# Start addresses at multiples of 64 bytes and three row pitches for the projection's operands

## The chip, the cores and the metric

One core of one Trainium2 chip runs the whole kernel. The metric is the device time of one execution in microseconds (us); the median of three runs of the kernel before is 1004.42 us, the lowest 1004.33, the highest 1007.7.

## What is computed

One decoder layer over 1040 positions (16 learned meta tokens, then 1024 tokens) of width 1024. Cut to what matters:

```python
h = rms_norm(h_res, pre_norm_g[i])
z = h @ w_in[i]                       # 1040 x 1024 times 1024 x 7328
(pv, pg, cq, ckv, kr, mg, cu, cg, sbcx, sg, gl) = split_cols(z)
y_a = (pool_mixer(pv, ...) * silu(pg)) @ w_out_pool[i]
y_b = (mla_attention(cq, ckv, kr, ...) * silu(mg)) @ w_out_mla[i]
y_c = (conformer_conv(cu, ...) * silu(cg)) @ w_out_conf[i]
y_d = (short_conv(sbcx, ...) * silu(sg)) @ w_out_sc[i]
m = sum(sigmoid(gate_k) * y_k)        # four gates out of gl
h_res = h_res + rms_norm(m @ w_o[i], post_norm_g[i])
return h_res[:, N_META:]
```

## The kernel before

All large products are done in float32r on numbers split into a high and a low part: each operand has a hi and a lo copy, and a product is three matmuls, hi by hi, hi by lo and lo by hi.

**The projection (first 650 us or so).** `h @ w_in` is done with a Winograd scheme of seven half-size products (28 pairs of column blocks, 256 columns each). The activations stand in seven operand tiles `HB[b]` of shape 128 x 2 x 4 x 528: 2 for hi and lo, 4 blocks of 128 channels (`k`), and a row of 528 columns, 512 tokens and 16 meta columns. A row is thus 2112 bytes. The seven are B11, B21, B22 (= a block of h), T1, T2, T4 (sums of blocks) and T3, which is also the block B12. The second half of the tokens has no meta tokens of its own, so the 16 meta columns of B22 and of T3 are filled with zeros by two memsets on POOL, right at the start. `product` streams one row of `HB[b]` at a time past a block of weights: for each `k` the three matmuls are (hi weights, hi row), (hi weights, lo row), (lo weights, hi row), so 12 in all.

`unit` does the seven products of one pair of column blocks into the PSUM banks `ps_pa` to `ps_pd`. 23 of the 28 pairs need the 1024 tokens alone and run it once with 512 columns. Five need the meta columns too (the list marks them `MT`); they run it twice, on columns 0 to 255 (256 of them) and on columns 256 to 527 (272). `plain` does the block `ckv`/`kr` without the scheme, in the same two stretches: for each of two halves of the tokens `j` and two column blocks `i`, two products of 12 matmuls.

**The attention (about 650 to 873 us)** runs eight heads in two halves of the queries; `ps_s` are the scores, `ps_o` the weighted sums, and between them the output products of three branches (`ps_y`) are put in as filler. `maxima` first computes the scores of one head with a block of 128 queries as weights, streaming the keys `kt` in pieces: 656 keys go in two pieces of 328, 784 in two of 392, 912 in two of 456. **The end (873 us on)** is the output product of the attention branch (`ps_u<-boM`) and the Winograd product with `w_o` (`ps_o`, `ps_u` with the tiles `wa` streaming).

**Order and places.** Nothing is issued when it is written down. Every operation is recorded (`Plan.record`, which is why nearly all lines of the profile say L330, the line from which all is issued) and put in order by a list scheduler, `Plan.flush`, with a cost for each operation; a matmul of n columns in float32r costs `max(108, n / 2.25 + 3)` ns there. A buffer that will lie where an earlier one lay may be written only after the earlier one's last use (`sl["after"]`, from `Plan.lay_out`).

`Pool.lay_out` gives every buffer its place in a partition's memory. Buffers of the pools on the left follow each other from byte 512 of the kernel's own area up, those on the right (`HB` in the projection, the tiles `cp` later) end at byte `SBUF` = 212832. Each buffer's size is rounded up to 32 bytes. Since 212832 = 3325 x 64 + 32 and the sizes on the right are all multiples of 64, the right side starts half of 64 bytes off a multiple of 64; on the left the constants take 736 bytes, and everything behind them starts at 512 + 736 = 1248 = 19 x 64 + 32. The area itself starts at a multiple of 64. So nearly all operands lie at 32 bytes past a multiple of 64. Exceptions are the identity matrix, some buffers of the last stage that lie behind a 32-byte tile (`rso`): `a`, `c11`, `c22`, `u2`, `g`, and slices that start at an odd column.

Of the kernel before, what the change touches and what calls it, by code (L numbers as in the profile page):

```python
# [21 lines left out]
F32 = mybir.dt.float32  # L22
F32R = mybir.dt.float32r
BF16 = mybir.dt.bfloat16
AF = mybir.ActivationFunctionType
ALU = mybir.AluOpType
# [4 lines left out]
P = 128  # L31
# [5 lines left out]
KH = KD // 2  # L37

SBUF = 212832
# [5 lines left out]
LH = 512 + NM  # L45
# [11 lines left out]
B11, B21, B22, T1, T2, T3, T4 = range(7)  # L57
# [7 lines left out]
def f(ap):  # L65
    return ap.bitcast(F32)
# [79 lines left out]
class Pool:  # L146
# [30 lines left out]
    def lay_out(self, start):  # L177

        for g in self.groups.values():
            g["one"] = -(-max(b.bytes for b in g["order"]) // 32) * 32  # L180
        size = sum(g["n"] * g["one"] for g in self.groups.values())
        at = start = start - size if self.space == "right" else start
        for tag, g in self.groups.items():
            if not g["slots"]:
                g["slots"] = [{"i": i, "live": None, "after": 0} for i in range(g["n"])]
                for sl in g["slots"]:
                    self.pool.tile([P, g["one"] // 4], F32, tag=f"{tag}_{sl['i']}", name=f"{tag}_{sl['i']}")
            for sl in g["slots"]:
                sl["place"] = (self.space, at, at + g["one"])
                at += g["one"]  # L190
        return start if self.space == "right" else at


# [242 lines left out]
def trunk_kernel(ctx, tc, a):  # L436
    nc = tc.nc
    plan = Plan(nc)
    PE, ACT, DVE, POOL, SP = (plan.engine(e) for e in ("PE", "ACT", "DVE", "POOL", "SP"))
    ctx.enter_context(tc.manual_schedule())  # L440

    def pool(stack, **kw):
        return plan.open(stack, Pool(plan, stack.enter_context(tc.tile_pool(bufs=1, **kw)),
                                     psum=kw.get("space") == PSUM,
                                     side="dram" if kw.get("space") == DRAM else kw.get("side", "left")))
# [4 lines left out]
    def copy(out, in_, scale=1.0):  # L450
        ACT.activation(out, in_, AF.Copy, scale=scale)

    def sub(eng, out, x, y):
        eng.tensor_tensor(out, x, y, op=ALU.subtract)
# [7 lines left out]
    def split(hi, lo, src, eng=None):  # L462
        copy(hi, src)
        sub(eng or POOL, lo, src, f(hi))
# [10 lines left out]
    def rsqrt_mean(out, ssq, n, eps=EPS):  # L475

        DVE.tensor_scalar(out, ssq, 1.0 / n, eps, op0=ALU.mult, op1=ALU.add)
        POOL.tensor_tensor(out, out, mhalf[:out.shape[0], :out.shape[1]], op=ALU.pow)
# [29 lines left out]
    one = ExitStack()  # L508
    hpool = pool(one, name="hb", side="right", reuse_waits="tile")
    HB = {}  # L510
    for b, name in ((B11, "B11"), (T2, "T2"), (T1, "T1"), (T3, "T3"), (B21, "B21"), (T4, "T4"), (B22, "B22")):
        HB[b] = hpool.tile([P, 2, KH, LH], F32R, name=name)
    psum = pool(one, name="psum1", space=PSUM, reuse_waits="tile")

    def bank(tag="x"):

        return psum.tile([P, 512], F32, tag=tag, bufs=2 if tag == "x" else 1, name=f"ps_{tag}")
# [45 lines left out]

    def product(ps, w, b, c0, n, start, stop):

        for k in range(KH):
            s = slice(c0, c0 + n)
            xh, xl = HB[b][:, 0, k, s], HB[b][:, 1, k, s]
            last = stop and k == KH - 1
            PE.matmul(ps, w[:, 0, k], xh, start=start and k == 0, stop=False, skip_group_check=True)  # L570
            PE.matmul(ps, w[:, 0, k], xl, start=False, stop=False, skip_group_check=True)
            PE.matmul(ps, w[:, 1, k], xh, start=False, stop=last, skip_group_check=True)
# [3 lines left out]
    def unit(w, c0, n, out, pump, early=False):  # L576
# [10 lines left out]
        def first():  # L587
            product(pa, w["A12"], B21, c0, n, False, True)
            with plan.ahead(EVAC):
                out(0, 0, pa, None, u3 if early else a_)  # L590
            pump()

        product(pa, w["A11"], B11, c0, n, True, True)
        with plan.ahead(EVAC):
            copy(a_, pa)
        pump()
        if early:
            first()
        product(pb, w["S2"], T2, c0, n, True, True)
        with plan.ahead(EVAC):  # L600
            add(DVE, u2, pb, a_)
# [19 lines left out]
    def plain(w, c0, n, out):  # L621

        for j, bs in enumerate(((B11, B21), (B12, B22))):
            for i, m in enumerate((P, 64)):
                ps = bank(("pa", "pb")[i])[:m, :n]
                for h, b in enumerate(bs):
                    product(ps, w[h][i], b, c0, n, h == 0, h == 1)
                with plan.ahead(EVAC):
                    out(i, j, ps, None, None)
# [8 lines left out]
    def pairs_of_halves(n, each, store):  # L638

        z = {}  # L640

        def out(i, j, ps, x, tmp):
            first = i not in z
            if first:
                z[i] = up.tile([P, 2, n], F32, tag="z", bufs=2, name="z")
            m = ps.shape[0]
            each(i, z[i][:m, j], ps, x, tmp)
            if not first:
                store(i, z[i][:m])
        return out  # L650
# [79 lines left out]
    def square(x_, t):  # L730
        n = x_.shape[0]
        ACT.activation(tp.tile([P, D], BF16, tag="whl", name="junk")[:n], x_, AF.Square, accum_out=ssx[:n, t:t + 1])

    def scaled(x_, t):
        n = x_.shape[0]
        for i in range(2):
            s = slice(512 * i, 512 * (i + 1))
            DVE.scalar_tensor_tensor(x_[:, s], x_[:, s], rsx[:n, t:t + 1], gB[i][:n], op0=ALU.mult, op1=ALU.mult)
# [35 lines left out]
    def meta():  # L774
        square(xm, 8)
        rsqrt_mean(rsx[:NM, 8:9], ssx[:NM, 8:9], D)
        scaled(xm, 8)
        pt = bank()
        for k in range(KD):
            PE.transpose(pt[:, NM * k:NM * (k + 1)], xm[:, P * k:P * (k + 1)], ident[:NM, :NM])  # L780
        b1, b2 = (pt[:, 64 * i:64 * (i + 1)].rearrange("p (k n) -> p k n", n=NM) for i in range(2))
        hm = up.tile([P, 2, KH, NM], F32, tag="a", name="hm")
        copy(hm[:, 0], b1)
        sub(DVE, hm[:, 1], b2, hm[:, 0])
        for b, src, eng in ((B11, b1, DVE), (B21, b2, DVE), (T2, b1, DVE), (T4, hm[:, 1], DVE)):
            split(HB[b][:, 0, :, 512:], HB[b][:, 1, :, 512:], src, eng)
        hi = HB[T1][:, 0, :, 512:]
        copy(hi, b1, scale=-1.0)
        DVE.scalar_tensor_tensor(HB[T1][:, 1, :, 512:], b1, -1.0, f(hi), op0=ALU.mult, op1=ALU.subtract)

    for b in (B22, T3):
        POOL.memset(f(HB[b][:, :, :, 512:]), 0.0)
    rows = [
        (R_GB, 32, a["gate_bias"][0].rearrange("(k p) -> k p", p=P)),
        (R_PS, 2, a["pool_scale"][0].rearrange("(k p) -> k p", p=P)),
# [24 lines left out]
    parts(2)  # L820
    parts(3)
    meta()
    plain(w_kv, *U0, out_kv[0])
    for t in range(2):
        sums_of(t)
# [3 lines left out]
    for t in range(2, 4):  # L829
        sums_of(t)  # L830
    plain(w_kv, *U1, out_kv[1])
    for t in range(2, 4):
        operand_of(T3, t, xt[t + 4][:, :512])
# [420 lines left out]
    at = pool(two, name="at", reuse_waits="tile")  # L1254
# [324 lines left out]
    for d in (0, 4, 1, 5, 2, 6, 3, 7):  # L1579
# [3 lines left out]
        for c in range(2):  # L1583
            t = th[:, 512 * c:512 * (c + 1)]
            py = bank("u")
            for k in range(4):
                b = boM[c][k]
# [20 lines left out]
    def half(name, bufs=4):  # L1608
        return ep.tile([P, 512], F32, tag=name, bufs=bufs, name=name)
# [71 lines left out]
    for t in range(4):  # L1681

        parts = [slice(0, 512)] if t < 3 else [slice(0, 256), slice(256, 512)]
        g = half("g", 1) if t == 3 else a_[t]
        for i, cols in enumerate(parts):
            ps = bank("u" if i == 0 else "o")[:, cols]
# [43 lines left out]
```

## Time and profile before

| | before |
|---|---|
| time, median of 3 | 1004.42 us |
| profiled execution's own time | 1007.16 us |
| its span | 1005.5 us |
| granted TensorE clock | 0.992 |
| PE busy | 985.0 us, 98% |
| PE weight load busy | 828.5 us, 82% |
| DVE, ACT, POOL busy | 679.9, 445.8, 689.3 us |

PE is TensorE, whose matmuls are records of some 160 ns more than the time from one start to the next, because they are pipelined. What a matmul costs is therefore read from the distance of starts. The profile's chain of work goes back from the last instruction to whatever released each step.

### The profile page before, as it was taken

The numbers are of one execution on the slowest core, as the hardware profiler recorded it, in microseconds if no ns is written. First come the engines' busy times: TensorE is split into PE (matmuls) and PEld (weight loads), VectorE is DVE, ScalarE is ACT, GpSimd is POOL, SyncE is SP. The second block draws the span as 40 slices with busy tenths as digits, with TensorE's granted clock in tenths as the row PEclk, the third lists the DMA queues.
The fourth block names the chain that finished last, engine by engine and source line by source line (L and its number), as shares of the span: only waits on it lengthen the run. The fifth ranks groups of instructions, "written<-read, shape, count | busy, mean of one in ns | idle before, by whom it ended". The sixth has DMA issues, their size and how long they took to land.

```text
span 1005.5 us, 15187 instructions
## 1 busy us (share of the span) xinstructions
PE 985.0 (98%) x5093; PEld 828.5 (82%) x5093; DVE 679.9 (68%) x1106; ACT 445.8 (44%) x895; POOL 689.3 (69%) x640
## 2 busy tenths in 40 slices
PE   9999999999999999999999999989999999999996
PEld 9999898889888888877877888868887888788885
DVE  6856794898699679744454453165777777898547
ACT  7632233343433455444443444215564656224632
POOL 6768767577575698777877666135569796647946
PEclk9999999999999999999999999998999999999999
DMA  7269756568676866866655656795758572773534
GB/s 249 76 203 311 235 168 187 194 190 284 209 265 218 287 210 177 250 198 204 199 165 194 202 155 180 272 268 157 229 149 256 176 232 75 251 251 100 189 100 167
DMA packets 126303, 203.13 MB, mean 202 GB/s; under 512 B 19651, under 2 KB 79162, under 8 KB 124881
## 3 DMA queue, kind: packets, MB, share of 16 engines
q1 hardware_dynamic: 121600, 185.38, 58.9%
q10 hardware_dynamic: 4336, 15.73, 4.1%
q8 instruction: 40, 0.66, 0.3%
q0 software_dynamic: 288, 1.05, 0.3%
q14 instruction: 39, 0.31, 0.1%
HBM read 128.40 MB, written 73.72 MB: 201 GB/s over the span
## 4 chain that ended last, share of the span: by engine, by line
PE 90%; DVE 4%; issue 2%; POOL 2%; DMA 1%; ACT 0%; SPq 0%; DVEq 0%; POOLq 0%; ACTq 0%
PE ps_pb L330 16%; PE ps_pa L330 15%; PE ps_pc L330 15%; PE ps_o L330 10%; PE ps_pd L330 7%; PE ps_u L330 7%; PE ps_s L330 7%; PE ps_y L330 7%; PE ps_x L330 4%; PE ps_w L330 1%; DVE op L330 1%; DMA kt<-kr 1%; DVE ps_w L330 1%; DVE a L330 1%; POOL S L330 0%
## 5 line engine op out<-in xcount | busy, mean ns | idle before, releaser
L330 PE MATMUL ps_pb<-T,S 128*128 128x512 f32 (+2 forms) x792 | 174.8, 363 | 0.1
L330 PE MATMUL ps_pa<-B,A 128*128 128x512 f32 (+2 forms) x792 | 172.8, 362 | 0.0
L330 POOL TENSOR_TENSOR S<-ss,S 128x512 fp32r<-128x512 f32 x84 | 113.6, 1364 | 65.0 <-ACT S L330 59.2
L330 PEld LDWEIGHTS ps_pa<-B,A 128*128 128x128 f32 x792 | 134.6, 188 | 24.4 <-issue 0.7
L330 PEld LDWEIGHTS ps_pb<-T,S 128*128 128x128 f32 x792 | 133.8, 188 | 24.4 <-issue 1.2
L330 POOL TENSOR_TENSOR A<-raw,A 128x512 fp32r<-128x512 f32 x84 | 114.0, 1365 | 49.1 <-ACT A L330 47.0
L330 POOL TENSOR_TENSOR pt<-p,pt 128x512 fp32r<-128x512 f32 (+4 forms) x112 | 102.2, 939 | 51.8 <-ACT pt L330 26.0
L330 DVE SCALAR_TENSOR_TENSOR ps_w<-conv,par,ps_w 128x512 f32<-128x512 f32 x116 | 87.2, 752 | 2.5
L330 PE MATMUL ps_pc<-T,S 128*128 128x512 f32 (+2 forms) x396 | 85.8, 361 | 0.5 <-DVE z L330 0.5
L330 PE MATMUL ps_pc<-B,S 128*128 128x512 f32 (+2 forms) x396 | 85.3, 361 | 0.0
L330 PE MATMUL ps_pd<-T,A 128*128 128x512 f32 (+2 forms) x396 | 84.5, 361 | 0.0
L330 PE MATMUL ps_y<-bo,whl 128*128 128x512 f32 x288 | 83.4, 409 | 0.3 <-DVE op L330 0.3
L330 ACT ACTIVATE p<-ps_s 128x512 f32<-128x512 f32 (+4 forms) x112 | 49.6, 443 | 74.9 <-PE ps_s L330 31.2
L330 ACT ACTIVATE S<-ss 128x512 fp32r<-128x512 f32 x84 | 50.8, 628 | 71.4 <-DVE ss L330 39.3
L330 PEld LDWEIGHTS ps_pd<-T,A 128*128 128x128 f32 x396 | 67.2, 188 | 12.0
L330 PEld LDWEIGHTS ps_pc<-B,S 128*128 128x128 f32 x396 | 67.2, 188 | 12.0
L330 PEld LDWEIGHTS ps_pc<-T,S 128*128 128x128 f32 x396 | 66.9, 188 | 12.3 <-DVE z L330 0.7
L330 PE MATMUL ps_o<-pt,vt 128*128 128x512 f32 (+4 forms) x336 | 75.0, 336 | 1.8 <-ACT ol L330 1.5
L330 PE MATMUL ps_s<-qt,kt 100*128 100x512 f32 (+4 forms) x336 | 68.3, 330 | 0.7 <-DVE qt L330 0.7
L330 ACT ACTIVATE A<-raw 128x512 fp32r<-128x512 f32 x84 | 52.4, 626 | 37.0 <-PE ps_pd L330 18.2
L330 PEld LDWEIGHTS ps_o<-pt,vt 128*128 128x128 f32 (+1 forms) x336 | 53.2, 174 | 16.1 <-ACT ol L330 3.3
L330 PEld LDWEIGHTS ps_s<-qt,kt 100*128 100x128 f32 (+1 forms) x336 | 55.2, 179 | 11.5 <-issue 0.9
(344 smaller groups left out, 1893.8 us busy)
## 6 DMA issues: line engine op xcount, KB each, us to landing
raw<-in_w_in_dram SPq DMA_DIRECT2D x56, 512.0 KB
th<-th SPq DMA_DIRECT2D x32, 512.0 KB
th<-z ACTq DMA_DIRECT2D x30, 512.0 KB
v<-vhl SPq DMA_DIRECT2D x16, 384.0 KB
qt<-q SPq DMA_DIRECT2D x16, 384.0 KB
vt<-v SPq DMA_DIRECT2D x8, 768.0 KB
bo<-bo SPq DMA_DIRECT2D x6, 1024.0 KB
kt<-k SPq DMA_DIRECT2D x8, 520.0 KB
```

The source lines that it names most:

```text
L330: getattr(self.handle[o["eng"]], o["op"])(*map(real, o["args"]), **{k: real(v) for k, v in o["kw"].items()})
```

## The change

Four things are changed.

1. `Pool.lay_out` rounds buffer sizes up to 64 bytes instead of 32, and the right side ends 32 bytes lower (a tile `end` of 32 bytes fills the gap), so that every buffer starts at a multiple of 64 bytes.
2. The rows of `HB[T3]` and `HB[B22]` shrink from 528 to 512 columns (2048 bytes): the zero columns are gone, and with them the two memsets. `product` and `plain` stop at column 512 for these two.
3. The rows of `HB[T1]` and `HB[T2]` grow from 528 to 544 columns (2176 bytes); the added 16 columns are not used. B11, B21 and T4 keep 2112 bytes. The seven tiles together take as many bytes as before.
4. Slices that ran to the end of a row (`512:`) now end at 528 (`512:LH`).

```diff
-            g["one"] = -(-max(b.bytes for b in g["order"]) // 32) * 32
+            g["one"] = -(-max(b.bytes for b in g["order"]) // 64) * 64
         size = sum(g["n"] * g["one"] for g in self.groups.values())
-        at = start = start - size if self.space == "right" else start
+        at = start = start - size - SBUF % 64 if self.space == "right" else start
...
+        if self.space == "right" and not self.base:
+            self.base = self.pool.tile([P, SBUF % 64 // 4], F32, tag="end", name="end")
...
-        HB[b] = hpool.tile([P, 2, KH, LH], F32R, name=name)
+        HB[b] = hpool.tile([P, 2, KH, {T3: 512, B22: 512, T1: 544, T2: 544}.get(b, LH)], F32R, name=name)
...
     def product(ps, w, b, c0, n, start, stop):
 
+        if b in (T3, B22):
+            n = min(n, 512 - c0)
+            ps = ps[:, :n]
...
-                ps = bank(("pa", "pb")[i])[:m, :n]
+                ps = bank(("pa", "pb")[i])[:m, :n if j == 0 else min(n, 512 - c0)]
...
-            each(i, z[i][:m, j], ps, x, tmp)
+            each(i, z[i][:m, j, :ps.shape[1]], ps, x, tmp)
...
-            split(HB[b][:, 0, :, 512:], HB[b][:, 1, :, 512:], src, eng)
+            split(HB[b][:, 0, :, 512:LH], HB[b][:, 1, :, 512:LH], src, eng)
...
-    for b in (B22, T3):
-        POOL.memset(f(HB[b][:, :, :, 512:]), 0.0)
```

More of the change, by code (lines that the diff above doesn't have):

```diff
@@ L785, in meta @@
         for b, src, eng in ((B11, b1, DVE), (B21, b2, DVE), (T2, b1, DVE), (T4, hm[:, 1], DVE)):
-            split(HB[b][:, 0, :, 512:], HB[b][:, 1, :, 512:], src, eng)
-        hi = HB[T1][:, 0, :, 512:]
+            split(HB[b][:, 0, :, 512:LH], HB[b][:, 1, :, 512:LH], src, eng)
+        hi = HB[T1][:, 0, :, 512:LH]
         copy(hi, b1, scale=-1.0)
-        DVE.scalar_tensor_tensor(HB[T1][:, 1, :, 512:], b1, -1.0, f(hi), op0=ALU.mult, op1=ALU.subtract)
-    for b in (B22, T3):
-        POOL.memset(f(HB[b][:, :, :, 512:]), 0.0)
+        DVE.scalar_tensor_tensor(HB[T1][:, 1, :, 512:LH], b1, -1.0, f(hi), op0=ALU.mult, op1=ALU.subtract)
     rows = [
```

## The prediction, made before the changed kernel ran

> **What bounds the kernel now.** I read the page first, then the chain of work that ended last in order of time, then TensorE's timeline in the stretches that the change touches. Two lines of the page:
>
> ```profile
> span 1005.5 us, 15187 instructions
> PE 985.0 (98%) x5093; PEld 828.5 (82%) x5093; DVE 679.9 (68%) x1106; ACT 445.8 (44%) x895; POOL 689.3 (69%) x640
> PE 90%; DVE 4%; issue 2%; POOL 2%; DMA 1%; ACT 0%; SPq 0%; DVEq 0%; POOLq 0%; ACTq 0%
> ```
>
> TensorE is busy for 98% and makes up 90% of the chain, about 905 us; all transfers together are 1% of it. The time changes when a matmul's step changes, or when one of the few places changes where TensorE waits. The chain in order of time has long pieces in which nothing but matmuls stands (start, length, count):
>
> ```profile
> 166.19 2.78 PE ps_pb L330 x12
> 667.20 9.62 DMA kt<-kr
> 873.24 44.62 PE ps_u L330 x192
> 917.86 22.30 PE ps_o L330 x96
> 940.16 22.31 PE ps_u L330 x96
> ```
>
> So a matmul of 512 columns steps by 2.78 / 12 = 231.7 ns in the projection, where rows are 2112 bytes apart, and by 22.31 / 96 = 232.4 ns (44.62 / 192 gives the same) at the end, where rows are 2048 bytes apart. That difference of 0.7 ns is the first hint on row pitch. Both are bound by the streamed row, not by the weights, since the step grows with the columns. This stretch of the timeline has products of 12 matmuls, first with 272 columns (a second stretch of an `MT` pair), then with 256 (the first stretch of the next):
>
> ```profile
> 126.97 1.68 PE L330 MATMUL ps_pb<-T,S 128*128 128x272 f32 x12
> 128.48 1.68 PE L330 MATMUL ps_pc<-T,S 128*128 128x272 f32 x12
> ...
> 134.54 1.68 PE L330 MATMUL ps_pc<-B,S 128*128 128x272 f32 x12
> 136.05 1.58 PE L330 MATMUL ps_pa<-B,A 128*128 128x256 f32 x12
> 137.47 1.58 PE L330 MATMUL ps_pb<-T,S 128*128 128x256 f32 x12
> ```
>
> From 126.97 to 136.05 stand six products of 272 columns (the row of the third to fifth is left out): 9.08 / 6 = 1.513 us each. The one of 256 takes 137.47 - 136.05 = 1.42 us, 118.3 ns a matmul. From 256 to 512 columns a step grows by 231.7 - 118.3 = 113.4 ns, 0.443 ns a column, which leaves about 4.9 ns that do not depend on the columns.
>
> **The meta columns of T3 and B22.** In the second stretch of the five `MT` pairs the products with T3 and B22 stop at 256 columns: 5 x 2 = 10 products. In `plain` it is the second half, two blocks by two column groups: 4 products. Each goes from 1.513 to 1.42 us, so 14 x 0.093 = 1.3 us come off. All of it lies on TensorE's own chain, in stretches such as the one shown where one product starts as the other ends; only the four of `plain`, 0.4 us, lie in the first 50 us, where TensorE also waits for transposes and could lose them again. So -0.9 to -1.3 us; I take -1.3.
>
> **The memsets.** POOL's rows at the start:
>
> ```profile
> 1.37 0.20 POOL L330 MEMSET B<- 128x128 f32 x1
> 1.51 0.20 POOL L330 MEMSET T<- 128x128 f32 x1
> 1.66 0.11 POOL L330 MEMSET conv<- 128x14 f32 x1
> 7.89 0.71 POOL L330 TENSOR_TENSOR rsx<-rsx,mhalf 128x2 f32<-128x2 f32 x1 [6.12 <-DVE rsx L330]
> ```
>
> They take 0.3 us and POOL is idle for 6.12 us behind them, waiting for DVE. Taking them away is worth nothing; without that idle time it would be 0.3 us.
>
> **The row pitch.** 23 full pairs stream 12 matmuls of 512 columns for each operand: 552 for T3 and B22 together, 552 for T1 and T2. T3 and B22 get the pitch of the last stage, 2048 bytes, whose step is 0.7 ns longer: 552 x 0.7 = +0.4 us. A pitch of 2176 bytes occurs nowhere in the trace. Its bounds are the nearest rows: 231.7 ns at 2112 and 232.4 at 2048, so 0 to +0.4 us; nothing excludes a small gain, and I allow the same 0.4 us below. As 2176 steps on from row to row, like 2112 and unlike 2048, I take 0. The engines that write these rows (ACT and DVE, out of the transposes) write the same bytes with another pitch, and their work is hidden behind the wait for x.
>
> **The start addresses.** This is the large question: all 5093 matmuls read operands that move by half of 64 bytes. The trace has both cases side by side. The first piece of the keys in `maxima` starts at the tile's own start, 32 bytes past a multiple of 64; the second starts 328, 392 or 456 columns on, which is 20.5, 24.5 or 28.5 times 64 bytes, and so exactly on a multiple of 64. Three pairs that ran back to back, each with the matmul behind it:
>
> ```profile
> 713.52 0.46 PE L330 MATMUL ps_s<-kt,qt 96*128 96x328 f32 x2
> 713.82 0.40 PE L330 MATMUL ps_y<-bo,whl 128*128 128x512 f32 x1
> ...
> 717.52 0.52 PE L330 MATMUL ps_s<-kt,qt 96*128 96x392 f32 x2
> 717.88 0.55 PE L330 MATMUL ps_s<-qt,kt 100*128 100x272 f32 x3
> ...
> 742.19 0.58 PE L330 MATMUL ps_s<-kt,qt 96*128 96x456 f32 x2
> 742.60 0.52 PE L330 MATMUL ps_s<-qt,kt 100*128 100x144 f32 x6
> ```
>
> The pairs take 0.30, 0.36 and 0.41 us. With 4.9 ns and 0.443 ns a column for both matmuls they would take 0.300, 0.357 and 0.414: the aligned piece is not faster than the other. The streamed row's address therefore costs nothing that this can see, some 3 ns a matmul. What the trace does not hold is a block of weights on a multiple of 64 bytes; there the bound is the 4.9 ns that do not depend on the columns, since the rest is proportional to the streamed columns: 0 to -5093 x 0.0049 = -25 us. I take 0, the row that is nearest.
>
> For the other engines the trace has both cases as well. DVE's convolution slides its start by 4 bytes from tap to tap, through every place within 64 bytes:
>
> ```profile
> L330 DVE SCALAR_TENSOR_TENSOR ps_w<-conv,par,ps_w x116: 733/756/757, 117.6 to 413.5; 128x512 f32<-128x512 f32 x116
> ```
>
> From shortest to longest that is 3%, with the median at the top: the start does not matter. In the last stage ACT squares tiles on multiples of 64 (`c`) and copies tiles off them (`wr`), and POOL multiplies `a` (on) and subtracts into `mh` (off):
>
> ```profile
> L330 ACT ACTIVATE wa<-wr 128x512 fp32r<-128x512 f32 x21 | 13.1, 627 | 13.9 <-DMA wr<-so 8.3 <-PE ps_u L330 3.3 <-POOL c L330 1.5
> L330 ACT ACTIVATE junk<-c 128x512 f32<-128x512 f32 x8 | 5.1, 633 | 6.7 <-DVE c L330 6.6
> L330 POOL TENSOR_TENSOR mh<-m,mh 128x512 fp32r<-128x512 f32 x4 | 5.2, 1295 | 0.0
> L330 POOL TENSOR_TENSOR a<-a,pgB 128x512 f32<-128x512 f32 x3 | 3.9, 1284 | 1.7 <-ACT junk L330 1.7
> ```
>
> 627 against 633 ns and 1295 against 1284: nothing there. For transfers I have no such pair, but TensorE waits for them in one place only (the row of the waits; the page's mean rate and the size of a common load are for a rival below):
>
> ```profile
> PE ps_s L330 <- DMA kt<-kr: 3.3, 1, 3.3
> ...
> DMA packets 126303, 203.13 MB, mean 202 GB/s; under 512 B 19651, under 2 KB 79162, under 8 KB 124881
> ...
> th<-th SPq DMA_DIRECT2D x32, 512.0 KB
> ```
>
> So faster transfers could give back 3.3 us at most, and the start.
>
> **The order.** The planner sees 168 matmuls cheaper by 16 / 2.25 = 7 ns and some places that end a few bytes later, so its list can come out with other neighbours. That costs or gives a little wherever TensorE waits; taken as 0, at most the 3.3 us of that one wait either way as long as no load changes its turn.
>
> [...] The three pairs say that 32 or 64 bytes make no difference. [...]
>
> **The sum.** -1.3 + 0.4 = -0.9 us. The profiled execution took 1007.16 us (span 1005.5, 1.7 around it), 2.7 above the median of 1004.42, within the runs shown (1004.33 to 1007.7). It would become 1006.3; the median 1003.5. Its own range is -1.7 to +0.1 from the columns and the pitch, widened by 3.3 both ways: 999 to 1008. A measurement here can tell about 0.5%, 5 us, from no change; this is inside.
>
> **Rivals.** *Aligned weights shorten each step.* The 4.9 ns go: 1004.4 - 25 = 979. For it speaks that they are not explained by columns; against it that the weights load beside the running matmul. Half of it would give 992. Should the part that grows with the columns fall as well, it would be more than 25 us; the three pairs speak against that for the streamed row. Chance 0.25, most of it between 979 and 999.
>
> *The second head's keys land later.* At the start of the attention the chain shows `kt<-kr`, a load of 9.62 us, and TensorE already waits 3.3 us for its end. Every microsecond by which SP's queue issues it later is then a microsecond of the whole time. If the changed places or the order put one or two loads of 512 KB ahead of it, at 202 GB/s (the page's mean) 2.6 us each, the median becomes 1006 or 1009. It decides from a delay of 6 us, some two such loads and the 0.9 us made good, which gives 1009.5. Chance 0.13 from that point on.
>
> *The change does not do what it says*: an address that stays off a multiple of 64. Then only the columns and pitch count, and the time is the forecast's: not a case of its own.
>
> **How the numbers follow.** Forecast 0.62, the first rival 0.25, the second 0.13. The first lies nearly all below 999.4, the second above 1009.4, the forecast's own range between. So faster 0.25, same 0.61, slower 0.14 (0.01 of the forecast's edge). The range runs from 979, which leaves about half of the first rival out, to 1010, which leaves some 0.08 out.
>
> **What would show it.** Right: products of 12 with 512 columns still at 2.78 us, with T3 and B22 at up to 2.79; ten products of a second stretch at 1.42 instead of 1.51 us; the last stage still at 22.3 us for 96. Wrong: 96 matmuls of the last stage at 21.8 us or less (the first rival, since only addresses changed there), products of T1 or T2 other than those of B11, or a longer wait at `kt<-kr`.

## The result and the profile after

The changed kernel takes 1005.76 us (median of 14 runs, 1002.35 to 1008.58), the kernel before 1006.44 (14 runs beside it; the first three of them gave the 1004.42 that the prediction started from). The ratio is 0.9998, 95% interval 0.9989 to 1.0007: no difference that can be measured. The profiled execution, though, took 1002.35 us against 1007.16 before, and its span is 4.9 us shorter. It is the fastest of the 14, so its own parts have to be read before it is believed. The page, busy times and shares of the chain:

```profile
span 1000.6 us, 15167 instructions
PE 978.3 (98%) x5093; PEld 823.7 (82%) x5093; DVE 687.6 (69%) x1106; ACT 444.5 (44%) x895; POOL 688.9 (69%) x638
PE 84%; DVE 6%; POOL 4%; issue 3%; DMA 2%; ACT 0%; SPq 0%; DVEq 0%; POOLq 0%; ACTq 0%
```

TensorE is still busy for 98%, but its share of the chain fell from 90% to 84%, and DVE, POOL and issue took that over: the chain now runs through places where TensorE waits for others. The chain in order of time (start, length, count):

```profile
193.30 2.80 PE ps_pb L332 x12
...
668.87 8.91 DMA kt<-kr
...
871.01 43.61 PE ps_u L332 x192
914.62 21.76 PE ps_o L332 x96
936.38 21.76 PE ps_u L332 x96
```

Before, the 96 matmuls of the last stage took 22.30 and 22.31 us, now 21.76: 226.7 ns a matmul where it was 232.4. In the projection, 12 matmuls of 512 columns still take 2.78 to 2.80 us on the chain, as before. The second stretches, in TensorE's timeline:

```profile
132.22 1.67 PE L332 MATMUL ps_pd<-T,A 128*128 128x272 f32 x12
133.73 1.60 PE L332 MATMUL ps_pc<-B,S 128*128 128x256 f32 x12
135.17 1.58 PE L332 MATMUL ps_pa<-B,A 128*128 128x256 f32 x12
```

The product of 272 columns takes 133.73 - 132.22 = 1.51 us and the shortened one behind it 135.17 - 133.73 = 1.44. From the waits of TensorE (total, times, longest), four rows; the last three have no counterpart before:

```profile
PE ps_s L332 <- DMA kt<-kr: 2.3, 1, 2.3
...
PE ps_x L332 <- DVE rs L332: 1.1, 1, 1.1
PE ps_y L332 <- DVE pd L332: 0.8, 1, 0.8
PE ps_pb L332 <- DVE u L332: 0.7, 2, 0.4
```

From the starts of the matmuls in the two traces the span divides as follows (us; stalls are what the matmuls of n columns in the projection's scheme take beyond 4.9 + 0.443 n ns, where that is over 14 ns):

| | before | after | difference |
|---|---|---|---|
| projection, from the first matmul on | 650.6 | 652.9 | +2.3 |
| of it: before the first product of the scheme | 53.5 | 52.3 | -1.2 |
| of it: stalls in the scheme | 6.1 | 9.9 | +3.8 |
| of it: the scheme's matmuls of 512 columns, without stalls | 448.0 | 448.6 | +0.6 |
| of it: those of 256 and 272 columns, without stalls | 102.5 | 101.7 | -0.8 |
| attention | 221.0 | 216.4 | -4.5 |
| last stage | 123.0 | 120.2 | -2.8 |

So three things happened. The projection lost 2.3 us though some of its matmuls became shorter, the last stage gained 2.8, and the attention gained 4.5. The attention's part is mostly not the change's: it goes with the granted clock right behind the wait for `kt<-kr`. Stretches of the trace with busy times of PE, PEld, DVE, ACT and POOL, then the granted clock, the DMA share and GB/s, first before:

```profile
674.00:677.00 3.00, 0.06 (x1) 0.09 (x1) 0.71 (x3) 0.00 (x0) 0.95 (x4) 0.87 0.95 263
677.00:680.00 3.00, 3.00 (x11) 2.85 (x12) 0.81 (x3) 0.00 (x0) 0.00 (x0) 0.50 0.74 212
680.00:683.00 3.00, 3.00 (x12) 2.48 (x11) 1.46 (x4) 0.60 (x1) 0.00 (x0) 0.50 0.01 4
683.00:686.00 3.00, 3.00 (x8) 2.32 (x8) 2.78 (x7) 0.80 (x2) 0.00 (x0) 0.50 0.00 0
```

and the changed kernel:

```profile
677.00:680.00 3.00, 2.08 (x8) 2.00 (x9) 0.81 (x3) 0.00 (x0) 0.00 (x0) 0.67 0.96 275
680.00:683.00 3.00, 3.00 (x17) 2.57 (x16) 0.93 (x2) 0.60 (x1) 0.00 (x0) 0.76 0.21 62
683.00:686.00 3.00, 3.00 (x15) 2.44 (x14) 2.90 (x9) 1.87 (x4) 0.54 (x1) 1.00 0.00 0
```

Before, the clock stands at 0.5 from the wait on for 10.24 us; after, for 3.41 us. In the slow stretch before, matmuls of 512 columns step by 427 ns, and right behind it by some 234: 45% of such time is lost, which for the 6.1 us more of it is some 3 us (before, TensorE still waited for the first 0.7 us of the slow stretch), and the shorter wait is 1 us more: 4 of the 4.5. A small part belongs to the change, since the matmuls `ps_y` that are put in as filler step by 229.9 ns where it was 232.3, some 0.7 us over 288 of them. Profiles of kernels with the same order as the changed one have 6.83 and 10.24 us of half clock, so its length differs from execution to execution. Without the attention the profiles differ by +2.3 - 2.8 = -0.5 us, which agrees with the medians (-0.7).

### The profile page after: what moved, and what is told of

Same layout as the page of the kernel before. It is cut to its first block, busy times and chain, and to the rows that moved or that the text cites. A ratio compares the mean times of both kernels' runs of the same rounds, so it can differ in the third digit from the quotient of the medians.

```text
span 1000.6 us, 15167 instructions
## 1 busy us (share of the span) xinstructions
PE 978.3 (98%) x5093; PEld 823.7 (82%) x5093; DVE 687.6 (69%) x1106; ACT 444.5 (44%) x895; POOL 688.9 (69%) x638
## 4 chain that ended last, share of the span: by engine, by line
PE 84%; DVE 6%; POOL 4%; issue 3%; DMA 2%; ACT 0%; SPq 0%; DVEq 0%; POOLq 0%; ACTq 0%
PE ps_pb L332 14%; PE ps_pa L332 14%; PE ps_pc L332 13%; PE ps_o L332 10%; PE ps_u L332 7%; PE ps_s L332 7%; PE ps_y L332 7%; PE ps_pd L332 6%; PE ps_x L332 4%; DVE ps_w L332 2%; PE ps_w L332 1%; DMA raw<-in_w_in_dram 1%; DVE ss L332 1%; DMA kt<-kr 1%; POOL S L332 1%
## 5 line engine op out<-in xcount | busy, mean ns | idle before, releaser
L332 PE MATMUL ps_pc<-B,S 128*128 128x512 f32 (+1 forms) x396 | 85.5, 361 | 0.5 <-DVE z L332 0.5
```

Of the source, the lines that this page charges most:

```text
L332: getattr(self.handle[o["eng"]], o["op"])(*map(real, o["args"]), **{k: real(v) for k, v in o["kw"].items()})
```

## The experiments

The question was why the last stage became shorter, and where that gain went. Two theories: *alignment* (operands at multiples of 64 bytes make a matmul shorter) and *distance* (what counts is that the streamed row and the weights start at the same place modulo some power of two). In the last stage before, the streamed `wa` start at 96 and the weights `mh` at 224 modulo 256; after, both at 192. For the loss, the theory was the scheduler: it sees cheaper products and writes another order.

**Matmuls alone.** A kernel that computes nothing of the layer: groups of 24 matmuls in the kernel's own pattern (hi, lo, hi row of a block), with one start moved at a time.

> A kernel of matmuls alone: of the layer it computes nothing and hands x back as the output. For each of 36 settings it runs 24 matmuls in float32r back to back, with hi and lo rows and weights in the order of the projection; only the start of the streamed rows, the start of the weights and the pitches differ. PSUM tiles carry the setting in their name, digits written as letters (A is 0, B is 1, to J for 9). Theory, distance: a matmul of 512 columns steps by 226.7 ns where the streamed row and the weights start at the same place modulo 256 or 512 bytes (24 in 5.44 us; rowA, all of the 'both' settings, even bothE at 4 bytes and bothDC at 32), and by some 232 ns (5.57 us) where they do not (rowDC to rowEIA, wtsDC and so on, pitch 2112 against weights at a fixed pitch), with rowCFG (256) telling 256 from 512. Rival, alignment: the step is 226.7 ns wherever both start at multiples of 64, whatever the distance, so rowGE, rowBCI and wtsGE are as fast as rowA and bothDC is slow. With 256 columns the theory expects a smaller gain of the same kind.

It ran for 201.54 us at clock 1.0. TensorE's timeline; names end in the start in bytes with letters for digits (A is 0, so `rowGE` is 64 and `rowCFG` 256); `row` moves the streamed rows alone, `both` rows and weights, `wts` the weights alone, `pitch` is the distance from row to row (2048 in the others). A group's time is the distance to the next start:

```profile
25.64 5.60 PE L65 MATMUL psrowA<-X,W 128*128 128x512 f32 x24
31.08 5.77 PE L65 MATMUL psrowDC<-X,W 128*128 128x512 f32 x24
36.69 5.67 PE L65 MATMUL psrowGE<-X,W 128*128 128x512 f32 x24
42.19 5.77 PE L65 MATMUL psrowJG<-X,W 128*128 128x512 f32 x24
47.80 5.76 PE L65 MATMUL psrowBCI<-X,W 128*128 128x512 f32 x24
53.40 5.76 PE L65 MATMUL psrowBJC<-X,W 128*128 128x512 f32 x24
...
64.59 5.63 PE L65 MATMUL psrowCFG<-X,W 128*128 128x512 f32 x24
70.06 5.67 PE L65 MATMUL psrowDCA<-X,W 128*128 128x512 f32 x24
...
92.35 5.86 PE L65 MATMUL psbothE<-X,W 128*128 128x512 f32 x24
98.05 5.70 PE L65 MATMUL psbothBG<-X,W 128*128 128x512 f32 x24
103.59 5.61 PE L65 MATMUL psbothDC<-X,W 128*128 128x512 f32 x24
109.04 5.63 PE L65 MATMUL psbothGE<-X,W 128*128 128x512 f32 x24
...
136.63 5.74 PE L65 MATMUL pswtsBCI<-X,W 128*128 128x512 f32 x24
142.21 5.61 PE L65 MATMUL pswtsCFG<-X,W 128*128 128x512 f32 x24
147.66 5.75 PE L65 MATMUL pswtsDIE<-X,W 128*128 128x512 f32 x24
153.25 5.75 PE L65 MATMUL pspitchCBBC<-X,W 128*128 128x512 f32 x24
158.83 5.71 PE L65 MATMUL pspitchCBHG<-X,W 128*128 128x512 f32 x24
164.38 5.65 PE L65 MATMUL pspitchCDAE<-X,W 128*128 128x512 f32 x24
169.87 5.60 PE L65 MATMUL pspitchCFGA<-X,W 128*128 128x512 f32 x24
175.31 5.70 PE L65 MATMUL pspitchCBBCwFHG<-X,W 128*128 128x512 f32 x24
180.85 3.02 PE L65 MATMUL psnCFGrowA<-X,W 128*128 128x256 f32 x24
183.71 3.02 PE L65 MATMUL psnCFGrowBCI<-X,W 128*128 128x256 f32 x24
186.56 3.04 PE L65 MATMUL psnCFGrowCFG<-X,W 128*128 128x256 f32 x24
```

Rows and weights in step: 31.08 - 25.64 = 5.44 us, 226.7 ns a matmul. Rows moved by 128 bytes, which keeps every start at a multiple of 64: 53.40 - 47.80 = 5.60, 233 ns. Moved by 256: 70.06 - 64.59 = 5.47, in step again. Both moved by 32, off the multiples of 64: 109.04 - 103.59 = 5.45, still in step. Weights alone by 128: 5.58, by 256: 5.45. This speaks against alignment to 64 and for a distance modulo 256. It is not the whole rule: rows moved by 64 take 5.50, a value between, and both moved by 16 take 5.54, so places within 32 bytes count too. Both moved by 4 take 98.05 - 92.35 = 5.70, the longest of all, where the distance theory had looked for 5.44: a miss. Row pitches of 2304 and 2560 bytes, multiples of 256, take 5.49 and 5.44, and one of 2112 takes 5.58: where rows and weights don't stay in step from row to row, the gain is gone. With 256 columns there is nothing at all: 183.71 - 180.85 = 2.86 and 186.56 - 183.71 = 2.85. The distance theory had looked for a smaller gain there, and missed again.

**The kernel before, its left side moved by 128 bytes,** which puts `wa` and `mh` in step and leaves their starts 32 bytes off:

```diff
+    const.tile([P, 32], F32, name="shift")      # behind const = pool(...), unused
```

> The kernel before with one unused buffer of 128 bytes ahead of all others on the left; nothing is aligned to 64, all stays 32 bytes off. In the last stage the streamed tiles on one side and the weights on the other now start at the same place modulo 512 (480 and 480; before 352 and 480). Theory, distance: 96 matmuls of the last stage take 21.76 us instead of 22.30, about 2.5 us less over 456 of them, and the fillers and the attention branch gain too; the projection stays at 2.78 us for 12. Rival, alignment: 22.30 us as before, no gain.

1002.32 us, ratio 0.9968 (0.9954 to 0.9982). From its chain:

```profile
870.78 43.57 PE ps_u L330 x192
914.35 21.76 PE ps_o L330 x96
```

The last stage has 21.76 us for 96 and takes 120.1 us, like the changed kernel's, with no other edit than an unused tile of 128 bytes.

**The changed kernel with the same 128 bytes,** which takes it out of step again and leaves every start at a multiple of 64:

```diff
+    const.tile([P, 32], F32, name="shift")      # in the changed kernel
```

> The changed kernel with the same unused buffer of 128 bytes; everything stays at multiples of 64. In the last stage the two sides now differ by 128 bytes modulo 512 (64 and 448), in the projection the rows of T3 and B22 start where the weights do (448 and 448; before the shift 448 and 320). Theory, distance: the last stage goes back to 22.3 us for 96, 2.5 us lost, and the products with T3 and B22 fall from 2.78 to 2.72 us, 46 x 0.06 = 2.8 us gained, so the total is about the same. Rival, alignment: last stage stays at 21.76, projection as it is.

1006.03 us, ratio 1.0015 (0.9999 to 1.003). From its chain:

```profile
916.54 22.30 PE ps_o L332 x96
```

All starts aligned, and 22.3 us. The two runs together settle the last stage: the distance sets the step, alignment to 64 does not.

**The addresses alone,** that is part 1 of the change with the rows left at 528 columns (the tile `end` is left out here):

```diff
-            g["one"] = -(-max(b.bytes for b in g["order"]) // 32) * 32
+            g["one"] = -(-max(b.bytes for b in g["order"]) // 64) * 64
-        at = start = start - size if self.space == "right" else start
+        at = start = start - size - SBUF % 64 if self.space == "right" else start
...
```

> The first part of the change alone: buffers at multiples of 64 bytes, while all rows keep 2112 bytes and the zero columns and memsets stay. The list of instructions comes out as in the kernel before. Theory, distance: in the last stage both sides start at 192 modulo 256, so 96 matmuls take 21.76 us and the time falls as with the shift by 128 bytes, ratio 0.996 to 0.998; the projection stays at 2.78 us for 12. Rival, that the addresses cost something elsewhere that eats the gain of the last stage: ratio 0.999 to 1.001.

1002.71 us, 0.9967 (0.9952 to 0.9982). Every engine has the same order as before, and the shares of the chain on its page are the same as before, PE 90%. From its chain:

```profile
914.79 21.76 PE ps_o L332 x96
```

**The rows alone,** parts 2 to 4 of the change with the rounding left at 32 (two of its places are shown):

```diff
-        HB[b] = hpool.tile([P, 2, KH, LH], F32R, name=name)
+        HB[b] = hpool.tile([P, 2, KH, {T3: 512, B22: 512, T1: 544, T2: 544}.get(b, LH)], F32R, name=name)
...
-    for b in (B22, T3):
-        POOL.memset(f(HB[b][:, :, :, 512:]), 0.0)
```

> The second part alone: the new row pitches, no zero columns, no memsets, but buffers at multiples of 32 bytes as before. The list scheduler sees the shorter products and puts some 1000 of 5062 matmuls at other places; the list is that of the changed kernel. Theory, order: the projection loses some 3 to 4 us in waits that the other order brings, against 1.3 us of columns, and the last stage stays at 22.30 us for 96, so slower: ratio 1.001 to 1.004. Rival, that the pitches and not the order cost the projection its time: also slower, but then the same list without the new pitches would not be.

1007.73 us, 1.0016 (1.0001 to 1.0031). The shares of its chain

```profile
PE 84%; DVE 6%; DMA 3%; POOL 3%; issue 3%; ACT 1%; SPq 0%; DVEq 0%; POOLq 0%; ACTq 0%
```

and the last stage in order of time

```profile
919.34 22.39 PE ps_o L330 x96
```

The one part gains 0.33%, the other loses 0.16%, though it takes work away. The mark that the changed kernel shows comes with the rows: the chain has 84% PE here and 90% in the run before, and stalls in the scheme are 10.6 us here and 6.2 there. The order is another as well: TensorE's list has 1028 of its 5062 matmuls (the profile has 5093 records of them) at other places than before, DVE's some 360 of 1106 instructions, SP's 262 of 591. The loss by the order is larger than 0.16%, because the new rows lie otherwise to the weights, and the 512-column matmuls of the scheme take 446.5 us without stalls where the kernel before needs 448.0.

**The changed kernel in the old order.** The products of T3 and B22 tell the scheduler their old width; what runs is the changed kernel's work at its addresses. The main lines:

```diff
     if b in (T3, B22):
+        plan.cols = n
         n = min(n, 512 - c0)
...
+        if eng == "PE" and self.cols:           # in Plan.record
+            cost = max(108, self.cols / 2.25 + 3)
```

> The changed kernel, but the list scheduler is told the old width (272 columns) for the shortened products, so that its list is that of the kernel before on every engine. Theory, order: the projection no longer loses its 3 to 4 us, and columns (1 us) and last stage (2.5 us) both remain: ratio 0.995 to 0.997, 3 to 5 us faster than the changed kernel. Rival, pitch: the projection stays as slow as in the changed kernel, ratio 0.999 to 1.001.

1001.29 us, 0.9952 (0.9939 to 0.9966). The shares of its chain, and the last stage in order of time:

```profile
PE 92%; DVE 3%; POOL 1%; DMA 1%; issue 1%; ACT 0%; SPq 0%; DVEq 0%; POOLq 0%; ACTq 0%
```

```profile
916.17 21.76 PE ps_o L334 x96
```

The order is the kernel before's, the stalls are back at 6.4 us, and 0.9998 becomes 0.9952: the order alone cost 0.46%, about 4.6 us. The profiled execution does not show that gain in its own time (1003.76 us, the longest of seven runs), since it waited 4.8 us for the keys and had 10.24 us of half clock; the median does.

**The projection in step as well.** The last kernel, with the weight blocks moved by 128 bytes, which puts them in step with T3 and B22:

```diff
+    tp.tile([P, 32], F32, name="shift")         # behind tp = pool(...), unused
```

> As the run with the old widths in the list, and one unused buffer of 128 bytes ahead of the projection's buffers on the left alone, so that its weights start at 192 modulo 256, as the rows of T3 and B22 do; the later stages keep their places. Theory, distance: products with T3 and B22 step by about 228 to 230 ns instead of 232, worth 1 to 3 us of 552 matmuls, the last stage keeps 21.76 us for 96: ratio 0.992 to 0.996. Rival: no further gain.

998.94 us, 0.9935 (0.9919 to 0.995). From its chain:

```profile
911.01 21.76 PE ps_o L334 x96
```

The projection took 648.0 us from the first matmul on where it took 650.0. B22's rows now step by 228.7 ns and T3's by 230.4 (232.0 and 231.7 in the changed kernel; means of 512-column matmuls without stalls): some of the 5 ns, not all. Its interval overlaps that of the kernel it was made from, but all four of its runs (998.59 to 999.45 us) are shorter than any of that kernel's seven (999.72 to 1003.76). A part of that can be the half clock, which lasted 3.41 us in this profile and 10.24 us in that one; the 2.0 us in the projection are free of it.

**The keys of the second head earlier,** in the kernel before, to take the wait and the half clock away. `load_kv` issues the loads of one head's keys and values:

```diff
+    load_kv(1)                                  # right behind load_kv(0)
...
-            if c == 0 and h + 1 < H:
+            if c == 0 and 0 < h < H - 1:
```

> The kernel before, with the keys of the second head asked for right after those of the first, at the start of the attention, and not behind the first block of scores. It tests where the spread of some 5 us between runs and the gap around 670 us come from: in every profile TensorE waits 2 to 5 us for these keys, and right behind that its granted clock stands at half for 3.4, 6.8 or 10.2 us. Theory: without the wait the clock does not fall, so the wait (3.3 us) and half of the slow stretch (1.7 to 5.1 us) are both saved, ratio 0.991 to 0.995, unless the list, which changes in the attention, brings other waits. Rival: the clock falls for another reason; then the wait alone is saved, ratio 0.996 to 0.998, and the dip stays.

1003.44 us (1001.12 to 1009.66), 0.9972 (0.9955 to 0.9989): less than the theory looked for, and inside the range of the rival. Its longest waits, and the stretch where the half clock was:

```profile
PE ps_y L330 <- DVE th L330: 2.0, 2, 1.6
PE ps_x L330 <- POOL rs L330: 1.5, 2, 0.8
```

```profile
670.00:675.00 5.00, 4.61 (x27) 3.73 (x28) 4.34 (x14) 2.98 (x9) 3.61 (x6) 1.00 0.54 175
675.00:680.00 5.00, 5.00 (x24) 4.12 (x23) 3.73 (x10) 3.14 (x6) 1.95 (x3) 1.00 0.35 80
680.00:685.00 5.00, 5.00 (x30) 4.02 (x29) 2.10 (x7) 4.68 (x11) 5.00 (x5) 1.00 0.36 127
```

In this profile the wait for the keys is gone, the clock stays at 1.0, and the attention takes 215.7 us instead of 221.0, though with a new wait of up to 1.6 us for DVE's `th`. But the profiled run is this kernel's fastest, and the median gained only half as much. The granted clock of the ten runs goes with their times: 0.998 in three (1001.12 to 1001.97 us), as in the profile, where it is down only behind the last matmuls; 0.995 or 0.996 in six (1002.91 to 1004.66) and 0.991 in one (1009.66). So in seven of them the clock was down for longer after all. Whether a wait went ahead of it there is not shown, since only the fastest has a profile. Wait and half clock go together in the ten profiles of the layer; that the earlier load keeps the clock up in every run does not follow.

**Both together,** the projection in step and the keys of the second head earlier (on the kernel with the old widths in the list):

```diff
+    tp.tile([P, 32], F32, name="shift")
...
+    load_kv(1)
...
-            if c == 0 and h + 1 < H:
+            if c == 0 and 0 < h < H - 1:
```

> The run with the projection's weights in step with the rows of T3 and B22, plus the earlier load of the second head's keys: the best of the parts together. If they add up, ratio 0.984 to 0.989, about 990 to 995 us; if the earlier load brings nothing, 0.993 as without it.

998.53 us, 0.9926 (0.99 to 0.9952). The gains did not add up: it is not better than the projection in step alone by anything the intervals show. In its profile, without half clock in the attention, the attention takes 217.5 us; in that of the projection in step, with the later keys and 3.41 us of half clock, it took 217.7.

## Why the prediction held, and where it did not

The forecast, no change with the median at 1003.5, held: the ratio is 0.9998. The median itself came to 1005.76, mostly because the 1004.42 that it was counted from was 1006.44 in 14 runs. But it held by luck: two errors, each about 3 to 5 us, cancelled.

**The start addresses: taken as 0, wrong.** The last stage gained 2.8 us, and the addresses alone 0.33%, 3.3 us. The failed step is the one from three pairs in `maxima` to every matmul. The pairs compared a streamed start on a multiple of 64 with one off it, in pieces of 328 to 456 columns; they did not ask how it stood to the weights. By the runs, alignment indeed gives nothing; the distance gives 5 ns at 512 columns (226.7 ns against 232 to 233) and nothing at 256 (119.2 in step, 118.8 at 128 bytes). That the trace showed 231.7 and 232.4 side by side and never less in a long stretch was no evidence: no long stretch of the kernel before had both starts in step. Single matmuls had. With rows 2112 bytes apart and weight blocks 512, the fourth row of every product in the projection starts where the weights do modulo 256, and by the starts of single matmuls in the trace before, the first of its three steps by 226 to 230 ns and the next one by 233 to 236. A row of the timeline that adds up all 12 hides this.

**The first rival** had its sign appear, 96 matmuls at 21.76, and its price for a matmul of 512 columns came out: the 4.9 ns of the sum went (512 x 0.443 = 226.8, and 226.7 was measured). That is a coincidence, because its mechanism did not hold. Aligned weights do not shorten the step (the changed kernel with 128 bytes more: 22.30), and the 4.9 ns are no fixed part of every matmul, as they stay at 256 columns: in step, 226.7 ns at 512 and 119.2 at 256 make 0.42 ns a column and 11.7 ns beside them. So it came off some five hundred matmuls of the last stage, and in part off the fillers, and not off 5093 (2.8 us over the 504 that the chain shows there, 5.5 ns each).

**The order: taken as 0 with 3.3 us for one wait as its bound, mis-sized.** It cost about 4.6 us (0.9998 against 0.9952), in the projection: stalls rose by 3.8 us in the profiles. The bound was put on the longest single wait in the trace. The loss came in five more stalls of over 0.2 us than the old order had (14 against 9, 8.4 us against 4.6), the longest 1.3 us, and no row of the trace before could show them. "As long as no load changes its turn" was the condition, and it did not hold: SP's list changed too.

**The columns: -1.3 us, right for the products, and not to be seen in the stage.** Shortened products take 1.42 to 1.44 us where 1.51 was the rule, and the ten of the scheme give 0.8 us of the 0.9 that the sum has for them. But in the profiles of the addresses alone and of the changed kernel in the old order, which have one order, the projection takes 650.05 and 650.00 us: 0.4 us went into longer steps at 512 columns, the rest into small amounts elsewhere. The medians of these two differ by 0.9967 - 0.9952 = 0.15%, 1.5 us, which the intervals leave open.

**The pitch: +0.4 us, and it was not there.** T3 and B22 step by 231.7 and 232.0 ns at 2048 bytes (before 232.0 and 231.7), T1 and T2 by 232.0 and 232.2 at 2176 (232.1 and 231.9). So the 0.7 ns that the prediction read between 2112 and 2048 is better put down to those starts than to the pitch: at 2112 the four rows of a product pass through four distances, one of them in step, while the last stage stood 128 bytes apart throughout. What did get longer are B11 and B21, whose row pitch the change leaves alone: 232.8 and 233.0 ns where it was 231.6 and 232.1, about 0.6 us. The sign that the prediction named, T1 or T2 unlike B11, thus appeared from B11's side. The longer steps are there in the old order (232.8 and 232.9) and not with the addresses alone (231.8 and 232.1), so they come with the rows; why stays open. **The memsets: 0,** and nothing contradicts it: the first product of the scheme began 52.3 us behind the first matmul, and 51.9 to 52.8 behind it in the other runs, with the memsets or without (53.5 in the profile before).

**The second rival,** keys that land later, did not occur in the changed kernel: the wait was 2.3 us, where it was 3.3. It varies between 2.3 and 4.9 in the eight profiles that have it.

**A term was missing,** the half clock behind that wait. The table of the profile before has it in a clock of 0.992, which the prediction passed over.

What stays open: why the distance counts; why T3 (230.4 ns), B22 (228.7) and the fillers `ps_y` (229.9) gain less from being in step than the last stage does; why T3 and B22, both 64 bytes from the weights in the run with the rows alone, step by 229.5 and 232.4 ns there, so that the distance from the weights is not the whole rule in the kernel either; and T1, T2, B11, B21 and T4 were not put in step, as their pitches step through the distances from row to row.

## What to carry to other kernels

Where long float32r matmuls bound a kernel, choose the places of streamed rows and weights so that their starts agree modulo 256 bytes, with row pitches that keep this from row to row, and measure it by the distance of starts in the timeline: an unused tile of 128 bytes was worth 0.3% here. An edit that makes an operation cheaper also tells a list scheduler something new, so run it once more with the old costs before its worth is judged. And take the clock in short stretches behind each wait before two profiles are compared.

## What was not expected of the hardware

A matmul of 512 columns steps by 226.7 ns when the rows and the weights start in step (228.7 to 230.4 in the projection), by about 232 to 233 when 128 bytes apart, and the difference falls to nothing at 256 columns (119.2 and 118.8 ns).

A wait of 2.3 to 4.9 us for one load came with the clock at 0.5 for 3.41, 6.83 or 10.24 us in every profile that had it, and in neither of the two that had no such wait. In the profile before, where matmuls of 512 columns step by 427 ns in the slow stretch and by some 234 right behind it, 9.5 us of TensorE's work lay in it: an estimate of 4.3 us lost, more than the wait of 3.3 us itself.
